# Fp32 encoder trunk with seven-product phases: first two groups interleaved, first weights split earlier, norm by columns

## The chip, the core and the metric

One core of a Trainium2 chip. The metric is the device time of one execution, in microseconds. TensorE does the matmuls, VectorE (DVE in the rows) and ScalarE (ACT) read and write both memories on the chip, GpSimd (POOL) does element-wise work, and SyncE (SP) issues most transfers.

## The reference

Two layers on x of 1024 tokens and 1024 features, each a token mixer and a squared-ReLU MLP, every one behind an RMS norm and added back to x; then a last norm. The mixer of the first layer is a retention, that of the second an attention over chunks. All is float32.

```python
def _rmsnorm(x, g):
    ...
    y = xf * lax.rsqrt(jnp.mean(xf * xf, axis=-1, keepdims=True) + EPS)
    return (y * g.astype(jnp.float32)).astype(x.dtype)
...
def _sqrelu_mlp(h, w1, w2):
    u = jax.nn.relu(h @ w1)
    return (u * u) @ w2
...
for i in range(DEPTH):
    hn = _rmsnorm(h, mix_norm_g[i])
    ...
        h = h + _retention(hn, ret_w_in[j], ret_gn_g[j], ret_w_out[j])
    ...
        h = h + _chunk_attention(hn, att_w_in[j], att_rel_bias[j], att_w_out[j])
    h = h + _sqrelu_mlp(_rmsnorm(h, mlp_norm_g[i]), mlp_w1[i], mlp_w2[i])
return _rmsnorm(h, final_norm_g)
```

The MLP widens 1024 features to 4096 and comes back to 1024.

## The kernel before, in words

x lies in h, eight blocks of 128 features by 1024 tokens, each block in two halves of 512 tokens (hf 0 and 1). An fp32 product is three matmuls: operand and weight are each split into a high and a low part (`split`, L133: a cast on ScalarE gives hi, a subtraction on VectorE gives lo), and `mm3` (L160) adds hi x hi, hi x lo and lo x hi in one PSUM bank.

In time order: retention and its output product up to 926 us; the first up-projection (`mlp_up`) to 1263; the first down-projection (`mlp_down`) to 1624; the attention in-projection to about 1907; attention and its output product to 2212; the second up-projection to 2561; the second down-projection and the last norm to the end.

The up-projections and the attention in-projection are seven-product phases. The output of a job is 256 features by 1024 tokens, a 2 x 2 of blocks, and Strassen's scheme in Winograd's form makes it by seven products of 512 x 128 x 512, that is 12 matmuls each, instead of eight. Product p needs an operand xh/xl of index p, sums of token halves and feature blocks, and a weight wh/wl, sums of weight blocks. The operands serve all jobs of a phase: 16 in an up-projection, 12 (q, k and v) in the attention. The order of a job's products is `SEVEN` = `EARLY` + `LATE` (L246): 1, 2, 6, 5, 7, 3, 4. Products 1, 6, 7 and 4 add up in one PSUM bank, A; 2 in B; 5 and 3 in C. The sum so far is copied out after 1, 6 and 5 (`s`, ScalarE) and added to a bank after 2, 7 and 3 (`c`, VectorE); 4 is the last read of bank A. `done` then scales by the norm's rB and stores the block.

How the phase is entered: `XNorm.block` (L281) is called for each finished block of the output product ahead; it squares the block for the norm (acc), and, once the four blocks of a feature pair j are there, makes the early operands 1, 2, 6 and 5. `late` (L299) makes 7, 3 and 4 for all j when the phase begins. Then `seven` (L345) loads the first weights (wr, 1 MB), POOL makes the sums wS, and `make` (L339) splits them, two products ahead of use. `Norm.finish` (L219) runs after the first product: matmuls with ones sum acc over the features into all rows, and a square root, a full-size reciprocal (L174) and three more steps give rB. The first norm of the program, with `col`, also makes a column form, rcol, by `col_rsqrt` (L180).

`mlp_down` goes through eight chunks of 512 hidden features. `splits` (L508 on) loads half a chunk (ur, 1 MB, one buffer) from uD, where the up-projection has stored it, and splits it in four blocks of uh/ul; for chunk 0 all this comes ahead of `down` (L421), which loads and splits w2 (wraw, whi, wlo).

The order on each engine is set when the program is built, by a scheduler; each engine then goes through its queue in order.

## Time and profile before

| | |
|---|---|
| median of 3 runs | 2948.78 us (2948.29 to 2948.98) |
| the profiled execution | 2945.81 us |
| its span | 2943.9 us |
| mean granted clock of TensorE | 0.968 |
| TensorE busy | 2754.1 us, 94% |
| VectorE busy | 1565.9 us, 53% |
| ScalarE busy | 1070.1 us, 36% |
| POOL busy | 661.3 us, 22% |

The span goes from the first to the last instruction of the core; 1.9 us of the execution lie around it. A granted clock of 1.00 is TensorE's upper level, 2.4 GHz; 0.5 is the lower one, 1.2 GHz; a value between is a mixture over the stretch. A matmul row of 0.39 us shows a pipelined instruction from start to modelled end; its successor starts some 0.225 us after it.

### The profile page before, as it was taken

How to read it: one execution, taken by the hardware profiler on the slowest of the kernel's cores; microseconds unless marked ns; L12 is line 12 of the kernel's file. 1: busy time of each engine (PE TensorE's matmuls, PEld its weight loads, DVE VectorE, ACT ScalarE, POOL GpSimd, SP SyncE). 2: the span in 40 equal slices, each digit the busy share in tenths (PEclk: the TensorE clock that was granted, in tenths of full speed). 3: DMA queues.
4: the chain of work that ended last, by engine and by line, in shares of the span. 5: the costliest groups of instructions: out<-in, count | busy, mean ns of one | idle time of the engine just before them, and what ended most of it. 6: DMA issues, size and time to landing. Idle time of an engine off the chain costs nothing.

```text
span 2943.9 us, 34310 instructions
## 1 busy us (share of the span) xinstructions
PE 2754.1 (94%) x12698; PEld 2275.5 (77%) x12698; DVE 1565.9 (53%) x2637; ACT 1070.1 (36%) x1906; POOL 661.3 (22%) x579
## 2 busy tenths in 40 slices
PE   8999999889996999989999599979995999899998
PEld 6788888778885788878888478769983888788887
DVE  6430123366657644444446856568888444444454
ACT  4011221233325444421214334478874444312122
POOL 4320000032214222200001322255544222100002
PEclk9999999999998999999999799989997999999999
DMA  4322232433210233232331255595611333333231
GB/s 133 108 89 84 99 123 90 153 115 102 80 48 29 91 113 111 101 122 93 107 102 49 76 169 164 142 217 150 170 48 58 113 110 109 113 101 107 87 106 72
DMA packets 246232, 313.01 MB, mean 106 GB/s; under 512 B 13128, under 2 KB 168880, under 8 KB 244016
## 3 DMA queue, kind: packets, MB, share of 16 engines
q1 hardware_dynamic: 244512, 307.87, 34.0%
q10 hardware_dynamic: 1552, 2.95, 0.4%
q8 instruction: 100, 1.64, 0.2%
q14 instruction: 68, 0.56, 0.1%
HBM read 222.64 MB, written 90.74 MB: 106 GB/s over the span
## 4 chain that ended last, share of the span: by engine, by line
PE 83%; DVE 8%; ACT 3%; DMA 2%; POOL 2%; issue 1%; SPq 0%; ACTq 0%; POOLq 0%; DVEq 0%
PE ps L164 17%; PE ps L166 17%; PE ps L165 17%; PE pA L166 5%; PE pA L164 5%; PE pA L165 5%; PE pC L164 3%; PE pC L166 3%; PE pC L165 3%; DVE xl L140 1%; PE po L1111 1%; PE pB L166 1%; PE pB L165 1%; PE pB L164 1%; PE pt L1099 1%
## 5 line engine op out<-in xcount | busy, mean ns | idle before, releaser
L448 DVE TENSOR_TENSOR h<-ps,h 128x512 f32<-128x512 f32 x368 | 252.6, 688 | 311.9 <-PE ps L166 310.6
L164 PE MATMUL ps<-uh,whi 128*128 128x512 f32 x960 | 376.1, 392 | 19.0 <-ACT whi L136 19.0
L136 ACT CAST whi<-wraw 128x1024 fp32r<-128x1024 f32 x132 | 139.0, 1053 | 668.2 <-PE ps L165 501.6
L166 PE MATMUL ps<-uh,wlo 128*128 128x512 f32 x960 | 375.7, 391 | 0.1
L165 PE MATMUL ps<-ul,whi 128*128 128x512 f32 x960 | 375.5, 391 | 0.0
L164 PE MATMUL pA<-xh,wh 128*128 128x512 f32 x704 | 279.5, 397 | 59.1 <-ACT wh L136 28.2
L166 PE MATMUL pA<-xh,wl 128*128 128x512 f32 x704 | 278.0, 395 | 23.8 <-DVE wl L140 23.8
L165 PE MATMUL pA<-xl,wh 128*128 128x512 f32 x704 | 277.9, 395 | 0.0
L212 POOL TENSOR_TENSOR acc<-acc,sq 128x512 f32<-128x512 f32 x70 | 99.7, 1425 | 772.8 <-ACT sq L211 768.2
L140 DVE TENSOR_TENSOR wlo<-wraw,whi 128x1024 fp32r<-128x1024 f32 x125 | 159.8, 1278 | 169.7 <-ACT whi L136 169.4
L164 PEld LDWEIGHTS ps<-uh,whi 128*128 128x128 f32 x960 | 181.5, 189 | 57.4 <-ACT whi L136 19.9
L166 PEld LDWEIGHTS ps<-uh,wlo 128*128 128x128 f32 x960 | 181.3, 189 | 39.0 <-DVE wlo L140 1.5
L165 PEld LDWEIGHTS ps<-ul,whi 128*128 128x128 f32 x960 | 181.6, 189 | 37.8
L164 PE MATMUL ps<-hhi,whi 128*128 128x512 f32 x512 | 203.3, 397 | 4.3 <-ACT whi L136 1.8
L164 PEld LDWEIGHTS pA<-xh,wh 128*128 128x128 f32 x704 | 134.5, 191 | 90.4 <-ACT wh L136 43.4
L166 PE MATMUL ps<-hhi,wlo 128*128 128x512 f32 x512 | 203.0, 396 | 1.2 <-DVE wlo L140 1.2
L165 PE MATMUL ps<-hlo,whi 128*128 128x512 f32 x512 | 202.9, 396 | 0.0
L140 DVE TENSOR_TENSOR wl<-wS,wh 128x512 fp32r<-128x512 f32 x176 | 123.2, 700 | 109.1 <-ACT wh L136 108.7
L166 PEld LDWEIGHTS pA<-xh,wl 128*128 128x128 f32 x704 | 134.1, 190 | 53.8 <-DVE wl L140 26.0
L136 ACT CAST wh<-wS 128x512 fp32r<-128x512 f32 x176 | 109.3, 621 | 138.3 <-PE pA L165 63.1
L165 PEld LDWEIGHTS pA<-xl,wh 128*128 128x128 f32 x704 | 134.5, 191 | 27.5
L335 POOL TENSOR_TENSOR wS<-wr 128x512 f32<-128x512 f32 x44 | 59.4, 1350 | 411.8 <-DVE wl L140 411.8
(236 smaller groups left out, 6035.6 us busy)
## 6 DMA issues: line engine op xcount, KB each, us to landing
wr<-in_mlp_w_dram SPq DMA_DIRECT2D x32, 1024.0 KB, 5.5
uD<-c SPq DMA_DIRECT2D x128, 256.0 KB, 2.0
ur<-uD SPq DMA_DIRECT2D x32, 1024.0 KB, 5.6
wraw<-in_mlp_w_dram SPq DMA_DIRECT2D x64, 512.0 KB, 3.5
wraw<-in_ret_w_in_dram SPq DMA_DIRECT2D x48, 512.0 KB, 4.2
kk<-kA SPq DMA_DIRECT2D x32, 512.0 KB, 8.7
wr<-in_att_w_in_dram SPq DMA_DIRECT2D x12, 1024.0 KB, 5.0
vS<-t SPq DMA_DIRECT2D x32, 256.0 KB, 2.0
```

The lines of the kernel that those rows point to most:

```text
L136: nc.scalar.copy(out=hi, in_=src)
L140: eng.tensor_tensor(out=lo, in0=src, in1=hi.bitcast(F32), op=ALU.subtract)
L164: nc.tensor.matmul(ps, lhsT=lh, rhs=rh, start=start, stop=False, skip_group_check=more)
L165: nc.tensor.matmul(ps, lhsT=lh, rhs=rl, start=False, stop=False, skip_group_check=more)
L166: nc.tensor.matmul(ps, lhsT=ll, rhs=rh, start=False, stop=stop, skip_group_check=more)
L212: nc.gpsimd.tensor_tensor(out=self.acc[hf], in0=self.acc[hf], in1=sq, op=ALU.add)
L335: nc.gpsimd.tensor_tensor(out=t, in0=a[1, 0], in1=a[0, 0], op=ALU.subtract)
L448: nc.vector.tensor_tensor(out=hv, in0=ps, in1=hv, op=ALU.add)
L1099: nc.tensor.transpose(pt[:, c - done:c - done + P], pr[:, (kb - k0) * P:(kb - k0 + 1) * P], ident)
L1111: nc.tensor.matmul(po[:, oc:oc + n], lhsT=T[hd, "v"][:, kb, :], rhs=t[:, off[kb]:off[kb] + n], start=i == 0, stop=i == len(seq) - 1)
```

## The change

1. Order: a job's products go 1, 2, 5, 6, 3, 7, 4, so that 4 comes behind 7 in the same bank. In the first two jobs of a phase the early products of both come first, then the late ones in turn (`steps`).
2. Weights: the class `Seven` takes the place of `seven`. `begin` loads the first weights and splits those of the first two products; `run_tail` calls it after the ninth step of the product ahead of the phase, so in the output product, or in the last chunk of the down-projection.
3. Operands: x2 and x3 are scaled and split without a raw tile in between (`scaled`). x7 is made as x4 was: from the high and low part of an operand that is there, with a subtraction on POOL. `late` is a generator, and `spread` hooks its twelve steps behind the second to the tenth product; the two halves of `finish` come behind the first and the second.
4. Norm: `finish` always makes the column form; rB then comes from it by four products with ones (`wide`), four transposes and a copy.
5. Down-projection: a load for each block (xr, 256 KB, four buffers) instead of each half chunk; thirteen pairs of uh/ul instead of eleven; chunk 0's splits stand behind the first weights of `down`.
6. Temporary tiles 9 for 8; the attention's bias rows are hooked behind product 15 of the phase's list.

```diff
-        return pl.tile([P, HT], dt, name=name, tag="tmp", bufs=8 if pl is plain.get("gp") else 5)
+        return pl.tile([P, HT], dt, name=name, tag="tmp", bufs=9 if pl is plain.get("gp") else 5)
...
+            pc = psp.tile([P, HT], F32, name="pc", tag="ps")
+            for t in range(4):
+                for i, z in enumerate((ah, al)):
+                    nc.tensor.matmul(pc[:, 2 * t:2 * t + 2], lhsT=z[:, t * P:(t + 1) * P], rhs=ones[:, 0:2], start=i == 0, stop=i == 1)
+            col_rsqrt(self.gp, pc, hf)
+            if row:
+                wide = tmp_tile(self.gp, "wide")
+                ps = psp.tile([P, HT], F32, name="pss", tag="ps")
                 for t in range(4):
-                    for i, z in enumerate((ah, al)):
-                        nc.tensor.matmul(pc[:, 2 * t:2 * t + 2], lhsT=z[:, t * P:(t + 1) * P], rhs=ones[:, 0:2], start=i == 0, stop=i == 1)
-                col_rsqrt(self.gp, pc, hf)
-            if row:
-                ps = psp.tile([P, HT], F32, name="pss", tag="ps")
-                nc.tensor.matmul(ps, lhsT=ones, rhs=ah, start=True, stop=False)
-                nc.tensor.matmul(ps, lhsT=ones, rhs=al, start=False, stop=True)
-                v = tmp_tile(self.gp, "vv")
-                nc.vector.tensor_scalar(out=v, in0=ps, scalar1=1.0 / D, scalar2=EPS, op0=ALU.mult, op1=ALU.add)
-                rsqrt_newton(tmp_tile(self.gp, "sd"), v, rB[:, hf * HT:(hf + 1) * HT])
-    EARLY, LATE = (1, 2, 6, 5), (7, 3, 4)
+                    sl = slice(t * P, (t + 1) * P)
+                    nc.vector.tensor_scalar(out=wide[:, sl], in0=ones.bitcast(F32), scalar1=rcol[:, 4 * hf + t:4 * hf + t + 1], scalar2=None, op0=ALU.mult)
+                    nc.tensor.transpose(ps[:, sl], wide[:, sl], ident)
+                nc.scalar.copy(out=rB[:, hf * HT:(hf + 1) * HT], in_=ps)
+    EARLY, LATE = (1, 2, 5, 6), (3, 7, 4)
...
+        def scaled(self, p, j, src, g):
+            hi, lo = self.hi[p][:, j, :], self.lo[p][:, j, :]
+            nc.scalar.activation(hi, src, AF.Copy, scale=g)
+            nc.vector.scalar_tensor_tensor(out=lo, in0=src, scalar=g, in1=hi.bitcast(F32), op0=ALU.mult, op1=ALU.subtract)
...
-            b11, b21, t1, t2 = (self.fresh() for _ in range(4))
+            b11, t1, t2 = (self.fresh() for _ in range(3))
             nc.scalar.activation(b11, b[0][0], AF.Copy, scale=g[0])
-            nc.scalar.activation(b21, b[1][0], AF.Copy, scale=g[1])
             x.split(1, j, b11)
-            x.split(2, j, b21)
             nc.vector.scalar_tensor_tensor(out=t1, in0=b[0][1], scalar=g[0], in1=b11, op0=ALU.mult, op1=ALU.subtract)
+            x.scaled(2, j, b[1][0], g[1])
+            x.split(5, j, t1)
             nc.vector.scalar_tensor_tensor(out=t2, in0=b[1][1], scalar=g[1], in1=t1, op0=ALU.mult, op1=ALU.subtract)
             x.split(6, j, t2)
-            x.split(5, j, t1)
...
+                x.scaled(3, j, b[1][1], g[1])
+                yield
+            for p, z in ((7, 0), (4, 1)):
+                for j in range(4):
+                    g, b = self.parts(j)
+                    src, q = (b[0][1], 3) if p == 7 else (b[1][0], 6)
+                    t = tmp_tile(gp, "t")
+                    nc.vector.scalar_tensor_tensor(out=t, in0=src, scalar=g[z], in1=x.hi[q][:, j, :].bitcast(F32), op0=ALU.mult, op1=ALU.subtract)
+                    nc.gpsimd.tensor_tensor(out=t, in0=t, in1=x.lo[q][:, j, :].bitcast(F32), op=ALU.subtract)
+                    x.split(p, j, t)
+                    yield
...
+            self.steps = ([(i, p) for i in range(2) for p in EARLY] + [(0, 3), (1, 3), (0, 7), (0, 4), (1, 7), (1, 4)]
+                          + [(i, p) for i in range(2, len(jobs)) for p in SEVEN])
+
+            self.sums = {(0, 5): [(0, 5), (0, 6), (0, 3)], (1, 5): [(1, 5), (1, 6)], (0, 3): [(1, 3)], (1, 3): [(0, 7)], (0, 4): [(1, 7)],
+                         (1, 4): [(2, 5), (2, 6)]}
+            for i in range(2, len(jobs)):
+                self.sums[i, 2] = [(i, 3), (i, 7)]
+                self.sums[i, 4] = [(i + 1, 5), (i + 1, 6)]
...
+            i, p = self.steps[s]
+            if s == 0:
+                self.load(0)
+            elif s == 2:
+                self.load(1)
+            elif (i, p) == (1, 7):
+                self.load(2)
+            elif i > 1 and p == 1:
+                self.load(i + 1)
+            for g, q in self.sums.get((i, p), ()):
+                if g < len(self.jobs):
+                    self.groups[g].sums(self.wr, (q,))
+            self.groups[i].make(p)
...
+    def spread(norm, xb, fin, more=()):
+
+        gen = norm.late(xb)
+        hooks = {s: [] for s in range(12)}
+        hooks[0].append(lambda: fin(0))
+        hooks[1].append(lambda: fin(1))
+        for i in range(12):
+            hooks[1 + (i * 3) // 4].append(lambda: next(gen))
+        for s, f in more:
+            hooks.setdefault(s, []).append(f)
+        return hooks
...
+    def run_tail(gen, at, seven):
+
+        for i, _ in enumerate(gen):
+            if i == at:
+                seven.begin()
...
-                raw = up.tile([P, 4, HT], F32, name="ur", tag="ur", bufs=1)
-                DMA.dma_start(out=raw, in_=uS[c][hf].rearrange("b p t -> p b t"))
+                raws = []
                 for b in range(4):
-                    a = up.tile([P, HT], F32R, name="uh", tag="uh", bufs=11)
-                    z = up.tile([P, HT], F32R, name="ul", tag="ul", bufs=11)
-                    split(raw[:, b, :], a, z)
+                    raw = xr.tile([P, HT], F32, name="xr", tag="xr", bufs=4)
+                    DMA.dma_start(out=raw, in_=uS[c][hf, b])
+                    raws.append(raw)
+                for b in range(4):
+                    n = seat[0] % SEATS
+                    seat[0] += 1
+                    a, z = ((up if n < 8 else upx).tile([P, HT], F32R, name=nm, tag=f"{nm}{n}") for nm in ("uh", "ul"))
+                    split(raws[b], a, z)
...
+            gen = down(dict(psp=psp, norm=norm if c == NB - 1 else None), src, 4, rhs)
+            if c == 0:
+                next(gen)
+                run(splits(0))
+            elif c == NB - 1:
+                return run_tail(gen, 8, at)
+            for i, _ in enumerate(gen):
+                if nxt and i >= 7:
...
-            norm = XNorm(2, gp, xa, xt, 10)
+            norm = XNorm(2, gp, xa, xt, 4)
             box.update(psp=psp, norm=norm)
-            run(tail)
+            run_tail(tail, 8, seven)
...
-        seven(ws, psp, gp, norm.x, jobs, {(0, 1): fin, (2, 1): bias_rows})
+        seven.go(wr, psp, gp, norm.x, spread(norm, xb, lambda hf: norm.finish(psp, hf), [(15, bias_rows)]))
```

What moves on the engines, at three places. First TensorE, in the middle of the first up-projection, at the end of product 7. In the names xh_6569 is the high operand of product 7, xh_6571 that of 3; pA and pC are the banks. Before:

```order
L164 MATMUL pA<-xh_6569,wh 128x512
L165 MATMUL pA<-xl_6570,wh 128x512
L166 MATMUL pA<-xh_6569,wl 128x512
L164 MATMUL pC<-xh_6571,wh 128x512
L165 MATMUL pC<-xl_6572,wh 128x512
L166 MATMUL pC<-xh_6571,wl 128x512
```

Product 3, in bank C, came behind 7. In the changed program (xh_6689 is the operand of 7, xh_6229 that of the next job's 1, in that job's own bank A, and xh_6691 that of 4):

```order
L164 MATMUL pA<-xh_6689,wh 128x512
L165 MATMUL pA<-xl_6690,wh 128x512
L166 MATMUL pA<-xh_6689,wl 128x512
L164 MATMUL pA<-xh_6229,wh 128x512
L165 MATMUL pA<-xl_6230,wh 128x512
L166 MATMUL pA<-xh_6229,wl 128x512
L164 MATMUL pA<-xh_6229,wh 128x512
L164 MATMUL pA<-xh_6691,wh 128x512
L165 MATMUL pA<-xl_6692,wh 128x512
```

Four matmuls of the next job's product 1 now stand between 7 and 4.

Second VectorE at the entry to the first up-projection. t is raw operand 4, xl_6574 its low part, wl<-wr the low parts of the first weights, ah the first step of `finish`. Before:

```order
L312 SCALAR_TENSOR_TENSOR t_6617<-h_86,gall,xh_6230 128x512
L140 TENSOR_TENSOR xl_6574<-t_6612,xh_6573 128x512
L312 SCALAR_TENSOR_TENSOR t_6622<-h_88,gall,xh_6230 128x512
L140 TENSOR_TENSOR xl_6574<-t_6617,xh_6573 128x512
L140 TENSOR_TENSOR wl<-wr,wh 128x512 x2
L140 TENSOR_TENSOR xl_6574<-t_6622,xh_6573 128x512
L140 TENSOR_TENSOR wl<-wS,wh 128x512
L138 CAST ah<-acc_6224 128x512
```

The first wl stood here, near the end of the late operands. In the changed program the first of them stands in the output product, whose results h are still being added:

```order
L140 TENSOR_TENSOR xl_6236<-xr,xh_6235 128x512
L482 TENSOR_TENSOR h_83<-ps,h_83 128x512
L140 TENSOR_TENSOR wl<-wr,wh 128x512
L482 TENSOR_TENSOR h_83<-ps,h_83 128x512
L297 SCALAR_TENSOR_TENSOR xr<-h_83,gall,xr 128x512
L140 TENSOR_TENSOR xl_6230<-xr,xh_6229 128x512
L140 TENSOR_TENSOR xl_6234<-xr,xh_6233 128x512
```

and the entry itself, from the last such addition on (xl_6688 is operand 3, c the first sum of a job comes eight rows further down):

```order
L482 TENSOR_TENSOR h_88<-ps,h_88 128x512
L266 SCALAR_TENSOR_TENSOR xl_6688<-h_82,gall,xh_6687 128x512
L300 SCALAR_TENSOR_TENSOR xr<-h_88,gall,xr 128x512
L266 SCALAR_TENSOR_TENSOR xl_6688<-h_84,gall,xh_6687 128x512
L266 SCALAR_TENSOR_TENSOR xl_6688<-h_86,gall,xh_6687 128x512
L140 TENSOR_TENSOR xl_6236<-xr,xh_6235 128x512
L138 CAST ah<-acc_6227 128x512
L266 SCALAR_TENSOR_TENSOR xl_6688<-h_88,gall,xh_6687 128x512
L140 TENSOR_TENSOR al<-acc_6227,ah 128x512
L140 TENSOR_TENSOR wl<-wS,wh 128x512
```

The weights now stand ahead of most operands, and operands 7 and 4 come later still, between products.

Third SyncE's queue at the start of the first down-projection. Before:

```order
L495 DMA uD_112<-c 128x512 x7
L511 DMA ur<-uD_105 128x4x512
L495 DMA uD_112<-c 128x512
L147 DMA wraw<-in_mlp_w_dram 128x4x256 x2
L511 DMA ur<-uD_105 128x4x512
```

In the changed program:

```order
L528 DMA uD_112<-c 128x512 x5
L147 DMA wraw<-in_mlp_w_dram 128x4x256
L552 DMA xr<-uD_105 128x512 x4
L147 DMA wraw<-in_mlp_w_dram 128x4x256
L528 DMA uD_112<-c 128x512
L147 DMA wraw<-in_mlp_w_dram 128x4x256
L528 DMA uD_112<-c 128x512
L552 DMA xr<-uD_105 128x512
```

The first load of a half chunk stood behind seven of the last chunk's stores; weights and four single blocks now stand behind five.

## Rows read from the trace of the kernel before

**Rows 1.** Page, part 4: engines' shares of the chain that ended last.

```profile
PE 83%; DVE 8%; ACT 3%; DMA 2%; POOL 2%; issue 1%; SPq 0%; ACTq 0%; POOLq 0%; DVEq 0%
```

**Rows 2.** Busy time by stretch; columns in the first line.

```profile
core 0: us, PE busy (x) PEld busy (x) DVE busy (x) ACT busy (x) POOL busy (x), PEclk, DMA share, GB/s
926.00:986.00 60.00, 32.40 (x125) 24.09 (x124) 51.55 (x60) 24.00 (x42) 22.59 (x16) 0.80 0.21 70
1000.00:1050.00 50.00, 50.00 (x222) 41.40 (x221) 22.94 (x36) 21.46 (x37) 15.27 (x12) 1.00 0.29 95
1263.50:1283.50 20.00, 10.37 (x33) 7.50 (x32) 9.34 (x13) 7.05 (x11) 0.00 (x0) 0.66 0.74 237
1624.00:1684.00 60.00, 29.01 (x104) 22.31 (x103) 52.01 (x61) 22.01 (x38) 20.33 (x14) 0.72 0.25 73
1712.00:1732.00 20.00, 13.85 (x56) 10.66 (x55) 6.83 (x13) 4.23 (x9) 0.15 (x1) 0.83 0.76 223
2212.50:2282.50 70.00, 35.36 (x116) 26.06 (x117) 61.87 (x71) 31.79 (x55) 31.73 (x20) 0.73 0.19 61
2561.50:2581.50 20.00, 10.51 (x36) 7.68 (x35) 9.34 (x13) 7.02 (x11) 0.00 (x0) 0.74 0.74 237
40.00:85.00 45.00, 42.11 (x182) 33.56 (x181) 30.75 (x50) 6.12 (x8) 22.67 (x16) 0.96 0.29 94
```

**Rows 3.** Waits of TensorE, 925 to 980: line <- releaser, total us, times, longest.

```profile
PE pA L164 <- ACT wh L136: 12.3, 1, 12.3
PE pA L166 <- DVE wl L140: 11.2, 1, 11.2
```

**Rows 4.** Waits of TensorE, 1630 to 1680.

```profile
PE pA L164 <- DVE xl L140: 13.4, 1, 13.4
PE pA L166 <- DVE wl L140: 10.3, 1, 10.3
```

**Rows 5.** Waits of TensorE, 2212 to 2275.

```profile
PE pA L164 <- ACT wh L136: 15.9, 1, 15.9
```

**Rows 6.** Waits of TensorE, 1263 to 1280.

```profile
PE ps L164 <- ACT whi L136: 9.6, 1, 9.6
```

**Rows 7.** Waits of TensorE, 2560 to 2580.

```profile
PE ps L164 <- ACT whi L136: 9.5, 1, 9.5
```

**Rows 8.** Timeline of ScalarE, 1262 to 1275: start, duration, instruction, [idle before <- releaser].

```profile
1270.26 2.18 ACT L136 CAST uh<-ur 128x512 fp32r<-128x512 f32 x4 [4.95 <-DMA ur<-uD]
```

**Rows 9.** Timeline of VectorE, 940 to 951.

```profile
940.88 0.68 DVE L140 TENSOR_TENSOR xl<-b,xh 128x512 fp32r<-128x512 f32 x1
941.48 0.74 DVE L312 SCALAR_TENSOR_TENSOR t<-h,gall,xh 128x512 f32<-128x512 f32 x1
...
942.74 1.75 DVE L312 SCALAR_TENSOR_TENSOR t<-h,gall,xh 128x512 f32<-128x512 f32 x1
...
945.24 1.75 DVE L312 SCALAR_TENSOR_TENSOR t<-h,gall,xh 128x512 f32<-128x512 f32 x1
```

**Rows 10.** Groups by line, 880 to 980: xcount | busy us, mean ns | idle before.

```profile
L174 DVE RECIPROCAL rB<-sd 128x512 f32<-128x512 f32 x2 | 6.7, 3346 | 0.0
```

**Rows 11.** Groups by line on VectorE, 57 to 63.

```profile
L177 DVE SCALAR_TENSOR_TENSOR rcol<-sdc,rcol 128x4 f32<-128x4 f32 x1 | 0.2, 164 | 0.0
```

**Rows 12.** Timeline of POOL, 940 to 951.

```profile
944.64 1.80 POOL L313 TENSOR_TENSOR t<-t,xl 128x512 f32<-128x512 f32 x1 [0.69 <-ACT xh L136]
```

**Rows 13.** Timeline of TensorE, 1048 to 1050.

```profile
1048.65 0.39 PE L166 MATMUL pA<-xh,wl 128*128 128x512 f32 x1
```

**Rows 14.** Timeline of VectorE, 1046 to 1051.

```profile
1049.13 0.69 DVE L391 TENSOR_TENSOR c<-pA,s 128x512 f32<-128x512 f32 x1 [1.32 <-PE pA L166]
```

**Rows 15.** Timeline of TensorE, 1828 to 1830.

```profile
1829.17 0.39 PE L166 MATMUL pC<-xh,wl 128*128 128x512 f32 x1
```

**Rows 16.** Timeline of VectorE, 1812 to 1834.

```profile
1829.52 0.69 DVE L929 TENSOR_TENSOR c<-c,dhi 128x512 f32<-128x512 f32 x1 [0.69 <-ACT dhi L928]
1830.13 0.69 DVE L391 TENSOR_TENSOR c<-pC,s 128x512 f32<-128x512 f32 x1
```

More of the change, by code (lines that the diff above doesn't have):

```diff
@@ new lines, in load, with ready @@
+        def load(self, i):
+            if i < len(self.jobs):
+                self.groups[i] = Group(self.wa, self.wr if i % 2 else self.wa, self.jobs[i][0])
+        def ready(self, s):
+            if s >= len(self.steps):
+                return
+            i, p = self.steps[s]
[11 more added lines that the diff above has]
+            self.groups[i].make(p)
@@ new lines, in begin, with go @@
+        def begin(self):
+            for s in range(self.AHEAD):
+                self.ready(s)
+        def go(self, wr, psp, gp, x, hooks=None):
+            self.wr = wr
+            names = {1: "A", 2: "B", 5: "C"}
+            held = {}
+            for s, (i, p) in enumerate(self.steps):
+                self.ready(s + self.AHEAD)
+                done = self.jobs[i][1]
+                if p in names:
+                    held[i, names[p]] = psp.tile([P, HT], F32, name="p" + names[p], tag=names[p], bufs=2)
+                bank = held[i, {1: "A", 6: "A", 7: "A", 4: "A", 2: "B", 5: "C", 3: "C"}[p]]
+                wh, wl = self.groups[i].w.pop(p)
+                for j in range(4):
+                    mm3(bank, (wh[:, j, :], wl[:, j, :]), (x.hi[p][:, j, :], x.lo[p][:, j, :]), p in names and j == 0, j == 3, p not in names)
+                if p in (1, 6, 5):
+                    held[i, p] = t = tmp_tile(gp, f"s{p}")
+                    nc.scalar.copy(out=t, in_=bank)
+                elif p == 4:
+                    done(1, 0, bank)
+                    self.groups.pop(i)
+                else:
+                    t = tmp_tile(gp, "c")
+                    nc.vector.tensor_tensor(out=t, in0=bank, in1=held[i, {2: 1, 7: 5, 3: 6}[p]], op=ALU.add)
+                    done(*{2: (0, 0), 7: (1, 1), 3: (0, 1)}[p], t)
+                for f in (hooks or {}).get(s, ()):
+                    f()
@@ new lines, in trunk_kernel, with freed @@
+    with ExitStack() as ph:
+        xr = pool(ph, "xrC", LEFT)
+        plain["wp"] = pool(ph, "weightsC", LEFT)
+        up = pool(ph, "upC", LEFT)
+        ux = ctx.enter_context(ExitStack())
+        upx = pool(ux, "upxC", LEFT)
+        psp = pool(ph, "psC", None, 8, PSUM)
+        norm = XNorm(1, gp, xa, xr, 4)
+        jobs = [qk_job(0, 0), qk_job(1, 0)] + [v_job(i) for i in range(4)]
+        for i in range(1, 4):
+            jobs += [qk_job(0, i), qk_job(1, i)]
+        def freed():
+            made.append(Seven(pool(xs, "wsevenAD", RIGHT), jobs))
+            return made[0]
+        made = []
+        mlp_down(psp, xr, up, upx, uD, I["mlp_w2"][0], norm, freed=lambda: (ux.close(), freed())[1])
+        seven = made[0]
@@ L956, in fin @@
-        def fin():
-            for hf in range(2):
-                norm.finish(psp, hf)
         def bias_rows():
```

233 lines of the change are left out of this document (87 added, 146 removed).

## Prediction

> **What bounds the kernel now.** I read the page first: TensorE carries 83% of the chain that ended last [rows 1]. So time can only be won where TensorE stands still, and I went on to the busy time by stretch [rows 2]. The reader is to see two kinds of stretch. Inside the seven-product phase, 1000 to 1050, there are 222 matmuls in 50 us, 0.225 us apiece, at the full granted clock: nothing to win there. At each entry to a phase far fewer matmuls run. Counting each stretch's length less its matmuls at 0.225 us, TensorE loses 60 - 28.2 = 31.8 us at the first up-projection (call it A), 12.6 at the first down-projection (B), 36.6 at the attention in-projection (C), 7.4 once more at 1712 to 1732 (C2), 43.9 at the second up-projection (E), 11.9 at the second down-projection (F). The sum is 144 us. VectorE (DVE in the rows) is busy 51.6 us of 60 in A, 52.0 of 60 in C and 61.9 of 70 in E, against 22.9 of 50 inside the phase: it is the limit at these entries. Then I asked who ended the waits. At A it is the first weight split (12.3 us) and its low part (11.2) [rows 3]; at C the last early operand (13.4) and the low weights (10.3) [rows 4]; at E the weight split again (15.9) [rows 5]. B and F are of another kind: one wait of 9.6 or 9.5 us [rows 6, 7]; ScalarE waited there for the uD load before it could split operands and weights [rows 8]. After it TensorE runs for a while at its lower level, 1.2 GHz: the granted clock is 0.66 and 0.74 over these two stretches [rows 2].
>
> **The sum is made** against the profiled execution, 2945.81 us; the median of the runs is 2.97 us higher, and I add that at the end.
>
> **First weights during the output product, two groups interleaved, late operands between products (A, C, E).** Before, VectorE makes all late operands and only then the first weight parts; the first product had nothing to run with for 23 us. Now the weights of products 1 and 2 are split in the output product, the late operands come after the early products are under way, and eight early products (8 x 12 x 0.225 = 21.6 us) cover them instead of four. VectorE's work itself hardly shrinks, so I cost the entry as VectorE's queue from the end of the output product until both groups are through:
> - early operands and evacuations still owed at A: about nine instructions at 0.6 us, 5.4 us (such a step has 0.68 us busy, and the starts at 940.88 and 941.48 are 0.60 apart) [rows 9].
> - x3: four at 0.66 = 2.6 us. x7 and x4: eight chains DVE, POOL, ACT, DVE. Such chains follow each other in 2.50 us (942.74 to 945.24) [rows 9]: 20.0 us. Before, only x4 was made in this way, so four subtractions move to POOL per entry.
> - norm: two reciprocals of 3.35 us go [rows 10]. In their place stand eight 128x128 products, some 128x4 steps, and, as before, the split of the squares. No row has the 128x128 form: it lies between the 128x4 step, 0.16 us [rows 11], and 0.6; I take 0.25, nearer by its size to a quarter of the large form. With the split some 6 us for both halves.
> - twelve weight parts at 0.6 = 7.2 us; 14 sums and scalings at 0.6 = 8.4 us; five POOL sums that hold VectorE back for 1.0 us each, as in the chain below, = 5 us.
>
> Together 54.6 us, of which TensorE needs 14 x 2.7 = 37.8 for its matmuls: A loses **16.8 us** instead of 31.8. Bounds: were POOL never in VectorE's way, the chains would cost 1.35 us and the sums nothing, some 40 us and a loss of about 8, counting TensorE's in-order waits; were the last four products to begin only after the last x4, about 24. I stay near the middle. C loses 4.8 more than A before and that difference stays, since its outputs take more VectorE steps: 21.6. E loses 12.1 more before, because VectorE is further behind at the end of the output product, and that debt stays too: 28.9. Gains: 15 at each.
>
> The exclusion is what the sum rests on. In the chain the subtraction on VectorE takes 0.74 us when POOL is idle, and 1.75 beside POOL's step; it ends at 946.99, 0.55 us after POOL's at 946.44 [rows 9, 12]. The Trainium skill, SBUF: State Buffer, section Who interferes with whom, speaks against the change here: a VectorE instruction with two SBUF inputs and a GpSimd instruction that reads SBUF shut each other out, and whichever came second waits to the end. The trace agrees, with the 1.75 us; by that rule the four new POOL steps at each of three entries cost 1.0 us of VectorE each, 12 us in all, and without it nothing.
>
> **First operands and weights of the down-projection loaded earlier (B, F).** The four 256 KB loads and the weights are now issued while the last group still runs; the 1 MB load, issued after it, goes. What hid nothing before is hidden by six products, 16 us, more than the 6.8 us from the phase's end at 1263.5 to the first split at 1270.26 [rows 8]. I leave 2.5 us at each for the last split and a short slow stretch: gains 10 and 9.5. If VectorE's or ScalarE's queue puts the splits behind the last sums, half of it stays. The 64 smaller loads have a chunk's time, and I cost them at nothing; if that cover failed, each chunk would wait for a load.
>
> **Start and C2.** At the start two reciprocals stand on the way to the first rope; that stretch loses 45 - 41 = 4.0 us [rows 2], of which I take 3. At C2 one more temporary buffer (9 for 8) and bias rows one step later: 4 of 7.4.
>
> **What it costs: product 4 directly behind 7.** Both write bank A. Product 4 may start only when the sum c of product 7 has been read; before, product 3 in another bank lay between. The last matmul of 7 starts at 1048.65 [rows 13] and c ends at 1049.13 + 0.69 [rows 14], 1.17 us later. Four matmuls of the next group's product 1 now stand between, so 4 would be due 1.13 us later. With 0.06 us to restart and 0.1 for the matmul behind a wait I take 0.2 us, for 28 groups: 5.6. At the attention jobs VectorE reads late: the last matmul of product 3 starts at 1829.17 [rows 15], but c starts at 1830.13, behind a subtraction that waited 0.69 us for ScalarE [rows 16], and ends 1.65 after it. There 0.7 us in ten groups: 7. The last group of a phase has no matmuls between: 1.1 us, three times: 3.3. The lower bound of the term is nothing, the upper three times as much, 48. I keep 16. The column norm puts 12 small TensorE steps per half where two full ones stood: 2.
>
> **Sum.** 3 x 15 + 10 + 9.5 + 3 + 4 = 71.5 or 72 gained, 18 lost: 54. 2945.8 - 54 = 2892; as a median **2895 us**.
>
> **Rivals.** (1) VectorE and POOL are the limit at A, C and E whatever the order: the entries cost what they cost before, and only B, F, start and C2 gain, 26.5 less 18. That gives 2940. For it speaks that VectorE was busy 86 to 88% there; against it that the work before was done with TensorE waiting, and eight products now lie over it. 0.14. (2) Slower: the bank wait between 7 and 4 in every group. It eats the 72 - 2 us when it reaches 70/41, 1.7 us: c read 1.5 us later than in [rows 14], or two to three VectorE instructions of 0.6 us ahead of it. With four of them (2.4 us more) the 41 groups cost 107 us, and the time is about 2985. For it: VectorE's queue is strictly in order, and in [rows 16] one instruction already stood ahead. Against: in the new order c of 7 stands directly behind a scaling that is ready. 0.08. (3) The entries go to their lower bound: A 8, C 11, E 18 and the bank wait costs nothing: 30 and 16 more, 2849. It needs VectorE's chains to overlap with POOL, against [rows 9, 12]. 0.10. That the change doesn't move the first weights I exclude: the order shows them ahead.
>
> **How the numbers follow.** The forecast has 0.68; its own ends are 2864 and 2926: the three entries 5 us better or worse each, and the bank wait nothing or doubled, 15 + 16 = 31 either way. The range reaches to rival 1 without taking all of it, and towards rival 3: 2862 to 2937. About 0.2% (6 us) can be told from no change. Faster: 0.68, 0.10 and some 0.08 of rival 1: 0.86. Within 0.2%: 0.06. Slower: 0.08.
>
> **What would show it.** A: the wait of 12.3 us gone, the first product starting within 1 us of the last output matmul, and waits of 2 to 6 us later, ended by low weights or by x7 and x4. B and F: no wait over 3 us and matmuls at 0.225 from the start. In the phase: one wait per group of some 0.1 us on c, ended by VectorE, larger at the attention jobs. I am wrong if VectorE is busy over 95% for 60 us after each entry (rival 1), or if that wait is over 1 us in each group (rival 2).

## The result, and the profile after

The changed kernel takes **2929.43 us** (2925.1 to 2939.48, 4 runs) against 2948.53 (2948.29 to 2948.98, 4 runs): a ratio of 0.994, with a 95% interval from 0.9914 to 0.9965. It is 19 us faster. The forecast was 2895, a gain of 54: the sign and the range held, the size did not. One execution of a kernel below (four edits, x7 raw) took 12959 us and is left out of its median.

The first profiled execution of the changed kernel was the longest of all its runs (2939.48). The rows below are from a second one, of 2927.09; where the first differs, that is said. TensorE's share of the chain that ended last is 82% now, for 83 in [rows 1]:

```profile
PE 82%; DVE 9%; ACT 4%; issue 2%; POOL 2%; DMA 2%; SPq 0%; ACTq 0%; POOLq 0%; DVEq 0%
```

The busy time by stretch, at the places of [rows 2]:

```profile
core 0: us, PE busy (x) PEld busy (x) DVE busy (x) ACT busy (x) POOL busy (x), PEclk, DMA share, GB/s
933.50:993.50 60.00, 45.26 (x170) 35.31 (x169) 53.22 (x71) 25.31 (x46) 33.30 (x22) 0.80 0.17 53
1000.00:1050.00 50.00, 50.00 (x220) 40.92 (x219) 23.26 (x35) 21.66 (x38) 16.44 (x12) 1.00 0.36 123
1270.50:1290.50 20.00, 19.14 (x84) 15.39 (x83) 14.75 (x22) 8.11 (x14) 0.00 (x0) 1.00 0.73 237
1619.50:1679.50 60.00, 42.55 (x164) 32.48 (x163) 51.27 (x72) 24.43 (x44) 28.95 (x20) 0.83 0.21 59
1709.00:1729.00 20.00, 13.19 (x56) 9.77 (x55) 8.25 (x16) 5.43 (x13) 3.83 (x3) 0.83 0.62 196
2207.70:2277.70 70.00, 45.71 (x174) 33.33 (x173) 64.69 (x86) 33.53 (x59) 40.95 (x26) 0.83 0.15 47
2553.00:2573.00 20.00, 19.13 (x84) 15.46 (x84) 14.97 (x22) 8.46 (x14) 0.00 (x0) 1.00 0.71 227
40.00:85.00 45.00, 37.50 (x163) 30.47 (x162) 21.02 (x46) 6.02 (x8) 22.20 (x16) 0.92 0.26 85
```

B (1270.5) and F (2553) are nearly full: 84 matmuls each in 20 us, where there were 33 and 36. The entries A (933.5), C (1619.5) and E (2207.7) run 170, 164 and 174 matmuls instead of 125, 104 and 116; much of the stretch is still empty. VectorE's busy time has hardly moved, 53.2, 51.3 and 64.7 us against 51.6, 52.0 and 61.9 in [rows 2], though it holds 71, 72 and 86 instructions now for 60, 61 and 71. POOL's has grown by 8.6 to 10.7 us at each. The start (40 to 85) has got worse, 163 for 182, and inside the phase there are 220 for 222.

These stretches end before all late products are through. A better measure of an entry: the time from the start of the last matmul ahead to the start of the 168th matmul of the phase's products (two groups), less 167 times 0.2267 us, the distance of successive starts in the middle of the phase. At A before, the last matmul ahead starts at 925.9 and the 168th of the phase 71.1 us later, so 33.2 us are lost.

| us lost | before | after | gain forecast | gain measured |
|---|---|---|---|---|
| A, two groups | 33.2 | 28.5 | 15 | 4.7 |
| C, two groups | 37.9 | 32.4 | 15 | 5.5 |
| E, two groups | 45.1 | 37.1 (first profile 40.9) | 15 | 8.0 (4.2) |
| C2, third and fourth group | 12.5 | 12.8 (17.7) | 4 | -0.3 (-5.2) |
| B and F, 20 us stretches | 12.6 and 11.9 | 1.1 and 1.1 | 10 and 9.5 | 11.5 and 10.8 |
| start: the last matmul of the output product, counted from matmul 100 | | 7.1 later (8.3) | 3 | -7.1 (-8.3) |
| groups 3 to 15 of an up-projection | 0.0 | 2.5 | -2.6 | -2.5 |

The longest waits of TensorE at A in the changed kernel (columns as in [rows 3]), then at E:

```profile
PE pc L227 <- DVE ah L138: 7.9, 1, 7.9
PE pA L166 <- DVE wl L140: 6.0, 2, 3.7
PE pA L164 <- ACT wh L136: 0.6, 1, 0.6
```

```profile
PE pA L164 <- ACT xh L136: 5.7, 2, 5.5
PE pA L165 <- DVE xl L140: 5.0, 2, 3.0
PE pA L164 <- ACT wh L136: 4.4, 1, 4.4
PE pc L227 <- DVE ah L138: 3.0, 1, 3.0
```

The waits of 12.3 and 11.2 us in [rows 3] are gone; TensorE starts 0.2 us after the output product. Instead it meets the norm's first small matmul, pc, in the middle of product 2 and waits 7.9 us for VectorE's ah, and later for low weights. What VectorE does there, and POOL beside it:

```profile
941.24 0.74 DVE L300 SCALAR_TENSOR_TENSOR xr<-h,gall,xr 128x512 f32<-128x512 f32 x1
941.90 2.42 DVE L266 SCALAR_TENSOR_TENSOR xl<-h,gall,xh 128x512 fp32r<-128x512 f32 x2
...
945.18 1.76 DVE L266 SCALAR_TENSOR_TENSOR xl<-h,gall,xh 128x512 fp32r<-128x512 f32 x1
946.86 1.77 DVE L140 TENSOR_TENSOR al<-acc,ah 128x512 fp32r<-128x512 f32 x1
948.55 1.75 DVE L140 TENSOR_TENSOR wl<-wS,wh 128x512 fp32r<-128x512 f32 x1
```

```profile
945.06 1.33 POOL L336 TENSOR_TENSOR wS<-wr 128x512 f32<-128x512 f32 x1 [1.95 <-issue]
946.46 1.61 POOL L338 TENSOR_TENSOR wS<-wS,wr 128x512 f32<-128x512 f32 x1
948.16 1.60 POOL L342 TENSOR_TENSOR wS<-wr,wS 128x512 f32<-128x512 f32 x1
```

Instructions that take 0.68 to 0.74 us alone take 1.75 or more beside each of POOL's sums. Low weights for which TensorE waits later are among them: a matmul that starts at 980.12 has waited 2.4 us for the following one, which ran beside one of POOL's subtractions and took 1.75 us.

```profile
978.32 1.75 DVE L140 TENSOR_TENSOR wl<-wS,wh 128x512 fp32r<-128x512 f32 x1
```

Behind the wait at pc, which begins at 937.4, the granted clock falls: from 943 to 956 it is 0.50, TensorE's lower level, and 30 matmuls run there:

```profile
943.00:956.00 13.00, 10.46 (x30) 8.02 (x31) 12.28 (x19) 2.47 (x6) 7.70 (x6) 0.50 0.26 81
```

In the kernel before, the stretch at that level is longer (23 us, 932 to 955), but TensorE stands for most of it and runs 11 matmuls.

At the start TensorE stands before the new transposes (first fence, waits of TensorE from 40 to 85). VectorE's timeline shows why: the column chain's first step, vc, is queued behind ah, which waits 5.22 us for POOL's sum of squares, and `wide` comes at the chain's end:

```profile
PE pss L235 <- DVE wide L234: 7.5, 2, 5.8
```

```profile
46.28 0.43 DVE L138 CAST ah<-acc 128x512 fp32r<-128x512 f32 x1 [5.22 <-POOL acc L212]
46.62 0.15 DVE L182 TENSOR_SCALAR vc<-pc 128x4 f32<-128x4 f32 x1
...
49.13 0.87 DVE L234 TENSOR_SCALAR wide<-ones,rcol 128x128 f32<-128x128 f32 x4
```

Inside the phase, in one of its groups, product 7's last matmul starts at 1016.07 (such a place before is in [rows 13, 14]), c follows 0.42 us later, and after four matmuls of the next group comes product 4, whose second matmul starts 0.61 us after the row before it begins, where two matmuls take 0.45: some 0.2 us per group, as forecast.

```profile
1016.07 0.39 PE L166 MATMUL pA<-xh,wl 128*128 128x512 f32 x1
...
1016.97 0.77 PE L164 MATMUL pA<-xh,wh 128*128 128x512 f32 x2
1017.58 0.40 PE L165 MATMUL pA<-xl,wh 128*128 128x512 f32 x1
```

```profile
1016.49 0.69 DVE L413 TENSOR_TENSOR c<-pA,s 128x512 f32<-128x512 f32 x1 [0.77 <-PE pA L166]
```

At C2 the wait is still there, and ScalarE's timeline shows whose it is. ScalarE issues the transfers of the bias rows; the sixteen for skew, which read the table, start 2.6 us after its last write is issued and take 10.2 us to issue, and the next casts stand behind them:

```profile
PE pB L164 <- ACT wh L136: 6.8, 1, 6.8
```

```profile
1703.42 0.32 ACTq L1031 DMA_DIRECT2D extd<-ext  x1
...
1705.97 10.21 ACTq L1036 DMA_DIRECT2D skew<-extd  x16
1716.22 0.37 ACT L989 CAST vt<-pv 128x256 fp32r<-128x256 f32 x1 [11.39 <-DMA skew<-extd]
```

The kernel before shows the same in ScalarE's timeline:

```profile
1710.33 10.08 ACTq L974 DMA_DIRECT2D skew<-extd  x15
1720.45 0.58 ACT L385 COPY s<-pC 128x512 f32<-128x512 f32 x1 [9.74 <-DMA skew<-extd]
```

### The profile page after: what moved, and what is told of

It reads as the page before. It is cut to its first block, busy times and chain, and to the rows that moved or that the text cites. A ratio compares the mean times of both kernels' runs of the same rounds, so it can differ in the third digit from the quotient of the medians.

```text
span 2937.7 us, 34754 instructions
## 1 busy us (share of the span) xinstructions
PE 2783.1 (95%) x12762; PEld 2283.6 (78%) x12762; DVE 1584.8 (54%) x2659; ACT 1065.0 (36%) x1888; POOL 678.6 (23%) x591
## 4 chain that ended last, share of the span: by engine, by line
PE 81%; DVE 9%; ACT 4%; DMA 2%; issue 2%; POOL 2%; ACTq 0%; SPq 0%; POOLq 0%; DVEq 0%
PE ps L165 17%; PE ps L164 17%; PE ps L166 17%; PE pA L164 5%; PE pA L165 5%; PE pA L166 5%; PE pC L166 2%; PE pC L165 2%; PE pC L164 2%; PE po L1170 1%; DVE xl L140 1%; PE pt L1158 1%; PE pB L165 1%; PE pB L166 1%; PE pB L164 1%
## 5 line engine op out<-in xcount | busy, mean ns | idle before, releaser
L166 PEld LDWEIGHTS ps<-uh,wlo 128*128 128x128 f32 x960 | 180.2, 188 | 37.1
L140 DVE TENSOR_TENSOR wl<-wS,wh 128x512 fp32r<-128x512 f32 x176 | 142.5, 810 | 67.0 <-ACT wh L136 66.1
L165 PEld LDWEIGHTS pA<-xl,wh 128*128 128x128 f32 x704 | 135.5, 193 | 33.3 <-DVE xl L140 5.8
```

The costliest lines, as they stand in the source:

```text
L140: eng.tensor_tensor(out=lo, in0=src, in1=hi.bitcast(F32), op=ALU.subtract)
L165: nc.tensor.matmul(ps, lhsT=lh, rhs=rl, start=False, stop=False, skip_group_check=more)
L166: nc.tensor.matmul(ps, lhsT=ll, rhs=rh, start=False, stop=stop, skip_group_check=more)
```

## The experiments

Each is an edit of the changed kernel, and each was timed beside the kernel before. Losses are in the measure above; A, C and E stand for the entries.

| kernel | median us | ratio to before (95%) | A | C | E |
|---|---|---|---|---|---|
| changed, again | 2928.9 | 0.9937 (0.9922 to 0.9952) | 28.5 | 32.4 | 37.1 |
| first norm by rows | 2925.6 | 0.9925 (0.9909 to 0.9942) | 28.0 | 32.6 | 38.3 |
| bias transfers spread | 2922.7 | 0.9913 (0.9898 to 0.9928) | 27.2 | 33.0 | 38.9 |
| entry's POOL work on VectorE | 2911.6 | 0.9881 (0.9866 to 0.9896) | 23.8 | 26.2 | 31.8 |
| old order from group 3 | 2922.8 | 0.992 (0.9903 to 0.9936) | 27.4 | 33.1 | 38.8 |
| norm later | 2942.2 | 0.9981 (0.9972 to 0.9991) | 30.5 | 41.5 | 41.4 |
| no interleaving | 2948.0 | 0.9998 (0.9988 to 1.0007) | 37.1 | 36.4 | 44.9 |
| weights asked for late | 2930.1 | 0.9938 (0.9923 to 0.9953) | 27.5 | 32.9 | 39.6 |
| entry norms by rows | 2948.5 | 1.0003 (0.9994 to 1.0012) | 34.0 | 40.0 | 43.2 |
| four edits | 2894.7 | 0.9819 (0.9806 to 0.9832) | 23.8 | 27.5 | 33.3 |
| four edits, x7 raw | 2895.3 | 0.9822 (0.9809 to 0.9835) | 21.7 | 28.7 | 33.5 |
| four edits, squares on VectorE | 2889.6 | 0.9801 (0.9788 to 0.9815) | 21.4 | 25.7 | 32.4 |

**The changed kernel again.**

> The changed kernel once more, as the base of the next three. Theory: TensorE loses at the same places as in the first profile of it. Lost time up to the end of the first two groups after the entry: about 28 us at the first up-projection, 33 at the attention in-projection, 41 at the second up-projection. The time lies between 2925 and 2940 us. Rival: these losses are chance of one execution and move by more than 5 us; then the spread of the runs comes from there. If they stay and the time moves, the spread comes from the start, up to the rope tables.

A and C repeat within 0.5 us; E moved by 3.8 and C2 by 5.0, so not all of the spread comes from the start.

**First norm by rows.**

```diff
-            norm.finish(psp, 0)
+            norm.finish(psp, 0, full=True)
...
-                        norm.finish(psp, 1)
+                        norm.finish(psp, 1, full=True)
```

With `full`, rB is made by the steps of the kernel before; here the column form is made as well.

> The first norm of the program makes rB by rows again (one sum over all rows, full-size reciprocal) beside the column form; all other norms stay by columns. Theory: the column chain ends in transposes, which stand in TensorE's queue and wait for VectorE, 5.8 and 1.7 us at the start of the changed kernel. By rows TensorE does not wait for the chain, so matmul 300 comes 6 to 8 us earlier (75.9 us after the start of the span instead of 83.7) and the whole is 6 to 10 us shorter. Rival: the reciprocals of 3.35 us are what costs at the start, as the prediction had it; then the kernel is as slow or up to 4 us slower than the changed one.

Of the waits of 7.5 us at `wide` nothing is left; TensorE waits 1.7 us for the rope (first line), as in the kernel before (second line).

```profile
PE ps L164 <- DVE rc L648: 1.7, 1, 1.7
PE ps L164 <- DVE rc L590: 1.7, 1, 1.7
```

The output product ends 5.9 us earlier (counted from matmul 100), the time is 3.3 us shorter (2928.9 less 2925.6). That the wait goes is shown; the 3.3 us are not clear of noise, since the intervals of the two ratios overlap. In the two profiled executions the gain is lost again where the edit changes nothing: 1.6 us before matmul 100, 1.1 about B, 2.2 at C2 and 1.3 at E.

**Bias transfers spread.**

```diff
-            for i in range(AH):
+
+        def bias_skew(i0):
+            for i in range(i0, i0 + 2):
...
-        seven.go(wr, psp, gp, norm.x, spread(norm, xb, lambda hf: norm.finish(psp, hf), [(15, bias_rows)]))
+        seven.go(wr, psp, gp, norm.x, spread(norm, xb, lambda hf: norm.finish(psp, hf), [(15, bias_rows)] + [(22 + i, lambda i=i: bias_skew(2 * i)) for i in range(AH // 2)]))
```

> The sixteen transfers that lay out the bias rows are issued two at a time behind eight products of the attention in-projection, instead of all sixteen at once behind one. Theory: ScalarE issues them, and casts and copies queued behind them wait for 16 us in the changed kernel; TensorE then stands still for 11 us. Spread out, this wait goes, and the time is 9 to 13 us shorter. Rival: the weights are late because of the load of 1 MB that shares the queues with them; then the wait stays at over 6 us and the time moves by less than 4.

ScalarE's wait for the transfers falls from one of 11.4 us to two, of 4.6 together, and TensorE's wait on weights there is gone:

```profile
ACT vt L989 <- DMA skew<-extd: 2.5, 1, 2.5
ACT wh L136 <- DMA skew<-extd: 2.1, 1, 2.1
```

C2 loses 8.6 us instead of 12.8 to 17.7, and the time is 6.2 us shorter: the cause holds, the size was put too high.

**POOL's work at the entries on VectorE.**

```diff
-                    nc.gpsimd.tensor_tensor(out=t, in0=t, in1=x.lo[q][:, j, :].bitcast(F32), op=ALU.subtract)
+                    nc.vector.tensor_tensor(out=t, in0=t, in1=x.lo[q][:, j, :].bitcast(F32), op=ALU.subtract)
...
-                    self.groups[g].sums(self.wr, (q,))
+                    self.groups[g].sums(self.wr, (q,), nc.vector if g < 2 else None)
```

> At the three entries the subtractions for operands 7 and 4 and the weight sums of the first two groups run on VectorE instead of POOL, 8 + 8 instructions of 0.6 us per entry. Theory: VectorE and POOL shut each other out while both read the same memory, a POOL step costs VectorE about 1.0 us and its own 1.3 us lie on the chain, so doing the work on VectorE is shorter: loss at the first entry 20 to 24 us instead of 28, and 12 to 20 us less in all three. Rival: POOL's work ran beside VectorE's; then VectorE gets 9 to 10 us more per entry, each entry loses 5 to 10 us more and the time grows by 15 to 30.

```profile
934.90:994.90 60.00, 45.35 (x186) 35.57 (x186) 50.18 (x92) 28.17 (x50) 8.82 (x7) 0.89 0.24 78
```

In 60 us of A VectorE now does 92 instructions in 50.2 us busy; with POOL beside it, it did 71 in 53.2. Twenty-one instructions more, and less time: that is 0.55 us each instead of 0.75. The same instructions have become shorter; two kinds of them at A, first in the changed kernel, then in this one (mean ns behind the comma):

```profile
L140 DVE TENSOR_TENSOR wl<-wS,wh 128x512 fp32r<-128x512 f32 x8 | 9.6, 1200 | 0.1
L140 DVE TENSOR_TENSOR xl<-t,xh 128x512 fp32r<-128x512 f32 x8 | 9.9, 1236 | 2.9 <-ACT xh L136 2.4
```

```profile
L140 DVE TENSOR_TENSOR wl<-wS,wh 128x512 fp32r<-128x512 f32 x8 | 5.5, 683 | 0.0
L140 DVE TENSOR_TENSOR xl<-t,xh 128x512 fp32r<-128x512 f32 x8 | 5.4, 684 | 0.4 <-ACT xh L136 0.4
```

The entries lose 4.7, 6.2 and 5.3 us less, 16.2 in all, and the time falls by 17.3, as the theory had it. So the exclusion is a part of an entry's price; 23.8, 26.2 and 31.8 us stay lost without most of it.

**Old order of products from the third group on.**

```diff
-                          + [(i, p) for i in range(2, len(jobs)) for p in SEVEN])
+                          + [(i, p) for i in range(2, len(jobs)) for p in (1, 2, 6, 5, 7, 3, 4)])
```

> From the third group on, the products of a job go 1, 2, 6, 5, 7, 3, 4 as before the change; all else is the changed kernel. Theory: product 4 behind 7 waits for the sum c, 0.19 us in each of 28 groups, more at the attention jobs and 0.8 us at the ends of the phases; with product 3 between, all this goes. From the end of the second group to the end of the phase the loss at the first up-projection falls from 3.6 us to under 0.5, and the time is 8 to 13 us shorter. Rival: the wait is an overlap of matmul records, and TensorE gets nothing back; the time moves by less than 3 us.

Groups 3 to 15 lose 0.0 instead of 2.5 us, in both up-projections, so the rival falls. Some of it goes again at the phase's end: from the last group to 84 matmuls into the down-projection the changed kernel loses 2.5 us, this one 3.0 and 4.3, since the first split of the down-projection is now late:

```profile
PE ps L164 <- ACT uh L136: 2.0, 1, 2.0
```

So 2.0 and 0.7 us are left at the up-projections, and 0.8 in the attention's groups 5 to 11. The median fell by 6.1, more than these places show and less than the 8 expected; in the profiled execution 3.5 us of it lie ahead of the first entry, where the edit changes nothing, and the intervals of the two ratios overlap.

**The norm later.**

```diff
-        hooks[0].append(lambda: fin(0))
-        hooks[1].append(lambda: fin(1))
+        hooks[3].append(lambda: fin(0))
+        hooks[5].append(lambda: fin(1))
...
+                if s == 3:
+                    kept()
```

`kept` is the scaling of the first result.

> At the entries the norm is summed four products later: the first half after the fourth product (the scaling of the first result is put behind it), the second half after the sixth. Theory A: TensorE stands 8 to 10 us at the norm's first small matmul, which it meets in the middle of product 2, because VectorE has not yet come to the squares; the early products of both groups could run in this time, so the loss after 48 matmuls falls from 16 to under 10 us, and each entry ends 4 to 8 us earlier, 10 to 20 in all. Theory B: VectorE is the limit, and what TensorE gains in the early products it loses again before the late ones: the loss after 48 matmuls falls, that after 168 stays within 3 us of 28, 33 and 37 to 41, and the time moves by less than 6.

The early products do gain: 11.1 us lost after 48 matmuls at A, for 16.1. After 168 it is 30.5, because low weights of the first group's product 4 now come 7.5 us late:

```profile
PE pA L166 <- DVE wl L140: 7.5, 1, 7.5
```

Theory A falls: the early gain is lost again. Theory B names the direction, not the size: C loses 41.5 us for 32.4, and the time is 13 us longer, where it allowed 6. TensorE's wait at pc was not the loss, only the place where it showed.

**No interleaving.**

```diff
-            self.steps = ([(i, p) for i in range(2) for p in EARLY] + [(0, 3), (1, 3), (0, 7), (0, 4), (1, 7), (1, 4)]
-                          + [(i, p) for i in range(2, len(jobs)) for p in SEVEN])
+            self.steps = [(i, p) for i in range(len(jobs)) for p in SEVEN]
...
-            hooks[1 + (i * 3) // 4].append(lambda: next(gen))
+            hooks[1 + i // 3].append(lambda: next(gen))
```

The edit moves more than the order: the late operands come behind the second to the fifth product instead of the second to the tenth, and the weight sums follow the new order.

> The first group runs alone: 1, 2, 5, 6, 3, 7, 4, and then the second; first weights early and all else as changed. Theory B (VectorE is the limit): four products cover the late operands instead of eight, but VectorE needs the second group's weights only later; the loss after 168 matmuls grows by 2 to 8 us per entry, the time by 6 to 20. Theory A (TensorE's early products are what hides): 21.6 us of cover become 10.8, each entry loses 10 us more, and the time is that of the kernel before or longer by up to 15.

The entries lose 8.6, 4.0 and 7.8 us more than in the changed kernel, and the time is that of the kernel before (2948.0). It lies where the two theories meet, at the upper end of B's range and the lower end of A's; the sum of 20 us is short of A's 30. What is certain: without the interleaving, and the places of late operands and sums that go with it, the whole net gain of the change is gone. The wait of 8.4 us is at the first group's product 4, which now has no product of the second group ahead of it:

```profile
PE pA L166 <- DVE wl L140: 8.4, 1, 8.4
PE pc L227 <- DVE ah L138: 7.9, 1, 7.9
```

**First weights asked for late.**

```diff
             if i == at:
-                seven.begin()
+                pass
...
             self.wr = wr
+            self.begin()
```

> The first weights are loaded and split when the seven-product phase begins, as before the change; the interleaving and all else stay. Theory: they take a load of 5 us and VectorE's queue at its fullest, so the first product starts 8 to 13 us after the last matmul ahead of it instead of 0.2 to 0.9; two thirds of it come back, as the later products find their operands ready: the loss after 168 matmuls grows by 2 to 5 us per entry, the time by 6 to 15. Rival: with VectorE the limit nothing changes after 168 matmuls (within 1.5 us), and the time stays within 4 us.

The first product still starts 0.2 to 0.7 us after the matmul ahead: the scheduler that orders the queues put the splits where they had been. In the trace the instructions of TensorE, VectorE, ScalarE and POOL stand in the order of the changed kernel, all of them, so this is a third timing of that kernel. It says nothing on what the early weights are worth; that stays open.

**Norms of the entries by rows.**

```diff
-            seven.go(wr, psp, norm.gp, norm.x, spread(norm, xb, lambda hf: norm.finish(psp, hf)))
+            seven.go(wr, psp, norm.gp, norm.x, spread(norm, xb, lambda hf: norm.finish(psp, hf, full=True)))
...
```

The attention's `seven.go` is changed in the same way; the column form is not made here.

> The changed kernel with the norms of the three entries by rows (one sum over all rows, full-size reciprocal), as before the change; the first norm of the program by columns. Theory: two reciprocals of 3.35 us and six full-size steps lie on VectorE, some 8 us more per entry than the column form, against waits of TensorE at the transposes of 1 to 2 us that go: each entry ends 2 to 6 us later, the time is 6 to 18 us longer. Rival: the column form costs at the entries what it cost at the start, and by rows the time is 3 to 8 us shorter.

All of the gain goes: 19.6 us more, with 5.5, 7.6 and 6.1 more lost at the entries. TensorE now waits four times for low weights:

```profile
PE pA L166 <- DVE wl L140: 11.5, 4, 4.1
PE pss L232 <- DVE ah L138: 8.9, 2, 7.9
```

The same form of the norm that costs at the start pays at the entries, where VectorE is the limit.

**Four edits together.**

> Four edits at once on the changed kernel: the first norm by rows, the old order of products from the third group on, the bias transfers spread, the entry's POOL work on VectorE. Theory: they act at different places and add up: 3.3 + 6.3 + 6.2 + 17.3 = 33 us less than the changed kernel's 2929, so 2896 (2888 to 2904). Rival: two of them stand on the same wait (the bias transfers and the order both act in the attention in-projection), and the sum falls short by 6 or more: 2902 to 2912.

They add up: 2894.7 against a sum of 2896. C2 loses 3.8 us, for 8.6 with the bias transfers spread alone.

**x7 as before the change.**

```diff
-                x.scaled(3, j, b[1][1], g[1])
+                b22, t3 = tmp_tile(gp, "b22"), tmp_tile(gp, "t3")
+                nc.scalar.activation(b22, b[1][1], AF.Copy, scale=g[1])
+                nc.vector.scalar_tensor_tensor(out=t3, in0=b[0][1], scalar=g[0], in1=b22, op0=ALU.mult, op1=ALU.subtract)
+                x.split(3, j, b22)
+                x.split(7, j, t3)
```

> The same, and operand 7 is made as before the change, from a raw scaled tile, without a second subtraction: four VectorE instructions of 0.6 us fewer per entry, one ScalarE instruction more for each; late operands are made one product later. Theory: VectorE is the limit at the entries, so each ends about 2.4 us earlier, the time is 4 to 8 us below that of the kernel with four edits. Rival: the late operands come too late or ScalarE's copies take the place; then it is no faster, or up to 6 us slower.

No difference (2895.3): A loses 2.1 us less, C 1.2 more, E stays. Four VectorE instructions fewer show at one entry of three.

**The squares on VectorE too.**

```diff
-                nc.gpsimd.tensor_tensor(out=self.acc[hf], in0=self.acc[hf], in1=sq, op=ALU.add)
+                eng = nc.vector if isinstance(self, XNorm) and m >= 4 else nc.gpsimd
+                eng.tensor_tensor(out=self.acc[hf], in0=self.acc[hf], in1=sq, op=ALU.add)
```

> The kernel with four edits, and the sums of the squares for the later four blocks (features 512 on) of the product ahead of each entry run on VectorE instead of POOL: eight instructions per entry. Theory: each POOL sum of 1.3 us, among VectorE's evacuations and splits, holds VectorE back for about 0.6 us, as much as the sum costs there, and the wait of 7.9 us at the norm's first small matmul gets shorter by 1 to 3 us, since the sums no longer wait for POOL: the time is 2 to 6 us shorter. Rival: at this place the two engines hinder each other less than a sum costs; then VectorE, the limit, ends later, the wait grows and the time is 3 to 10 us longer.

```profile
PE pc L228 <- DVE ah L138: 3.8, 1, 3.8
```

The wait at pc falls from 7.9 to 3.8 us, and the median by 5.1: **2889.6 us**, 1.99% below the kernel before, the lowest of all. The step from the four edits is not clear of noise: the two intervals overlap, and in the profiled execution the entries lose 5.0 us less but C2 3.3 more.

## Why the prediction was right or wrong

- **What bounds the entries: right in the main.** VectorE was named as the limit of A, C and E, and moving work between VectorE and POOL changes the time there. Its own sign for rival 1, VectorE over 95% busy, did not come: 89, 85 and 92% in the stretches above.
- **The entries: this is the step that failed.** The prediction costed an entry as VectorE's queue without a gap, 54.6 us at A. Some 14.2 of these were POOL's hindrance: eight chains at 2.50 us instead of 1.35, and five sums at 1.0. Measured are 66.4 us, from the last matmul ahead to the 168th: 59.0 busy in 77 instructions and 7.4 idle (first row; the second is the run with POOL's work on VectorE).

```profile
933.39:999.75 66.36, 51.29 (x194) 39.60 (x193) 58.98 (x77) 28.15 (x51) 35.45 (x23) 0.82 0.18 54
934.72:996.33 61.61, 46.97 (x193) 36.88 (x192) 51.02 (x93) 28.91 (x51) 9.00 (x7) 0.89 0.24 77
```

The second row has the same 77 instructions and 16 of POOL's steps. At 0.6 us these are 9.6, so the 77 take 41.4 us where POOL has seven steps left. That gives, as an estimate, three parts of the 11.8 us that were missing: VectorE's own work 41.4 for 40.4 (54.6 less 14.2); POOL's hindrance 17.6 (59.0 less 41.4) for 14.2, since 23 POOL steps run there and thirteen were priced; and 7.4 idle, priced at nothing. Most of the idle time is a wait for ScalarE's casts:

```profile
DVE xl L140 <- ACT xh L136: 4.6, 4, 1.4
```

That the two engines shut each other out, which the prediction read off [rows 9, 12], is borne out. The Trainium skill, SBUF — State Buffer, section Who interferes with whom, states it for a VectorE instruction with two SBUF inputs, and the trace agrees: 1.2 us in the mean instead of 0.68 for the eight wl.
- **The same from TensorE's side.** At the three entries together, gaps of over 0.6 us between matmuls fell from 97.4 to 65.0 us. Of these 32.4 us, 7.7 went to matmuls that start 0.3 to 0.6 us apart, 120 now for 69, most of them 0.43 apart as at the lower clock; 6.4 went to the norm's small steps and the rest. 18.3 remain of a forecast of 45. The prediction counted the lower clock at B and F only, and the longest new wait at A, 7.9 us at pc, it did not name. What the entries would take at the upper clock no run here tells.
- **"that debt stays too" at E, and the difference at C: right in kind.** C loses 3.9 more than A and E 8.6 more (forecast 4.8 and 12.1).
- **B and F: right.** 11.5 and 10.8 us gained, 10 and 9.5 forecast, and the granted clock is 1.00 in both stretches. The smaller loads cost nothing, as assumed: over the first 600 matmuls of each down-projection no more is lost than over the first 84, 1.3 us.
- **The start: wrong sign.** The prediction counted the two reciprocals that go and missed that the transposes stand in TensorE's queue: in the kernel before TensorE waited there for the rope (1.7 us) and for low weights (1.2), not for VectorE's column chain. 7.1 us lost for 3 gained; the run with rows takes the wait away.
- **C2: wrong.** A temporary buffer was not what it waited for. The bias transfers hold ScalarE; that was to be read from ScalarE's timeline of the kernel before, and was not.
- **Product 4 behind 7: right in sum.** In each up-projection it is 2.5 us for groups 3 to 15 and 1.1 for the last one. In the attention's groups 0.7 us each was too much: 7.1 us are lost from the fourth group's end to the eleventh's, against 4.7 before, and 0.8 of the difference goes with the old order. The last attention group loses 4.9 us, where 1.1 was priced: TensorE waits 2.9 us for c, and its next matmuls start up to 0.43 us apart. In the old order it loses 0.3, but TensorE then waits longer for the attention's first load, of kk: 19.1 us for 15.0, and 15.7 in the kernel before. So some 3.7 us more are lost there than before in either order; no term names this wait, and what sets its end was not tried. In all, the gains came to 33 us for 71.5, and these costs to 13 for 16; the two spans differ by 18.6.
- **The rivals.** Rival 2 did not come: the wait stayed at 0.2 us. Rival 1 came halfway: the entries gained 4.7, 5.5 and 8.0 us, neither nothing nor the 15 forecast. That the time lies inside the range is no success of the sum: the entries fell short by 27 us.

## What to carry to other kernels

Where two engines exclude each other, count every step of the slower one in the stretch, whatever it is for, before pricing a change of order; here handing POOL's work back to the busiest engine made the kernel faster. A busy engine's queue is not without gaps: here VectorE, the limit, stood idle for 7.4 of 66.4 us. A reduction that ends in matmuls or transposes puts its whole chain into TensorE's queue: here it paid at the entries, where TensorE waits anyway, and cost at the start, where it did not. Moving the place of a wait is no gain while the same engine owes the same work.

## What was not expected

VectorE did 92 instructions in less time than 71. The same column norm was worth 19.6 us at three entries and held up the output product by 5.9 us at the start. And the changed kernel's runs spread over 14 us, those of the kernel before over 0.7 in the same comparison and 2.8 to 5.4 in the others; C2 and E move between executions (12.8 or 17.7, 37.1 or 40.9 us), and why was not tried.
